# A hybrid attention and retention layer: one set of four transposes a group for dilation 1, and moved loads and splits at the stage borders

## The chip, the cores and the metric

The kernel runs on one core of a Trainium2 chip. The metric is the device time of one execution in microseconds (us). The core has five engines with an instruction queue each, which work in parallel and wait for one another by semaphores: TensorE (PE in the profile; its weight loads PEld), VectorE (DVE), ScalarE (ACT), GpSimd (POOL) and SyncE (SP), which only issues transfers. DVE, ACT and PE can reach PSUM, the memory that TensorE writes; in this kernel POOL works on SBUF alone.

## The reference

One layer for 4096 positions of width 1024, in float32. The input is normalised (RMS) and projected; of the result, eight heads of 64 go through dilated sliding-window attention, four heads through retention. Both are gated (SiLU), joined, projected and added to the input, and a last RMS norm follows. What the change touches is one branch of the attention, and how the branches are joined:

```python
DILATED_BRANCHES = ((128, 1), (512, 4), (2048, 16))      # (window, dilation)
...
    s = jnp.einsum('bhrnqd,bhrnkd->bhrnqk', qb, kb) * (Dh ** -0.5)
    dist = steps + qi - kj
    band = (dist >= 0) & (dist <= steps)
...
    p = jnp.exp(s - m)
    den = jnp.sum(p, axis=-1, keepdims=True)
    o = jnp.einsum('bhrnqk,bhrnkd->bhrnqd', p, vb) / den
    lse = (m + jnp.log(den))[..., 0]
...
    w = jax.nn.softmax(jnp.stack(lses, axis=0), axis=0)
    o = jnp.sum(w[..., None] * jnp.stack(outs, axis=0), axis=0)
```

Each block of 128 queries sees its own 128 keys (distance 0 and up) and the 128 before them (distance down to and including 128 steps). Since the branches are weighted by their denominators, the joined output is a sum over all three branches of unnormalised weights times v, divided by the sum of these weights. For a query and a key column of the same number, the key in the own block is at distance 0, that in the block before at distance 128; for every other column exactly one of the two is inside the window of dilation 1.

## The kernel before

The work has three stages, and each engine's instructions stand in the order in which the code issues them (`manual_schedule`).

**Projections** (`phase1`, line 115). Blocks of 512 positions are multiplied by the weights; each float32 operand is split into a high and a low part, so that `mm3` (lines 44 to 50) makes three matmuls of one product. Rotated q, k and v go to DRAM (`dr_q`, `dr_k`, `dr_r`, `dr_v`). For the last block the first loads of the next stage are issued in between: chunk 0 of the input (`load_x_chunk`, line 423), k of head 0 (`load_k`, lines 439 to 447), and chunk 1.

**Attention and retention** (`phase2`, line 544). Attention goes through 8 heads of 24 groups: 4 of dilation 1, 8 of dilation 4, 8 of dilation 16, 4 of dilation 1, so that eight groups of dilation 1 stand together at each change of head. A group is four blocks of 128 queries in two banks of two. `attention()` (line 818) issues one bank a slot: the scores S of a bank (`qk_bank`, 667); one slot later the exponentials on ACT (`exp_row`, 695) with the negated maxima that DVE found (`row_max`, 688, which also adds the mask); one more slot later four transposes of P on TensorE (`t_bank`, 704; three where there is no block before) and the copy of the transposed bank into the tile `pt`, bank 0 by DVE (716), bank 1 by ACT (714); at the fourth slot after the group's first the products with v (`pv_group`, 737), and then ACT's copy of the output. For dilated groups q is gathered four slots ahead, one half on POOL and one on DVE (643, 648). In each group the tile `pt` holds eight 128x128 blocks: for each block of queries the transposed weights of the block before and of the own block.

Between the slots `filler()` (1021) puts pieces of work by their TensorE cost: for each of 32 chunks of 128 positions the retention (scores 923, outputs, state, group norm 982 to 1002) and a part of the V products (L48 to L50 with tile V, whose epilogue `vch` is line 1037). It brings work to POOL (`hc`, the low part of the input chunk, 435; `rkl`, 908; `qbd`, 911; `qg`, 937; `rs`, 999) and to DVE and ACT. At the end gate weights are split (`split`, 76 to 88) and the first gates run.

**Output** (`phase3`, line 1134). For blocks of 256 positions: gates (`gate`, 1182, exponential in 1190), the joined and weighted attention (`mix`, 1193 to 1217), the split of the result (38 to 41), the output projection with `wo`, and the last norm. The weights of the branches (`branch_weights`, 498 to 528) come from the maxima and denominators of all heads, which `end_head` transposes into the tile `st`, `store_stats` (783) writes to DRAM (`dr_st`) and `load_stats` (786 to 796) reads back, three slots later, into `raw`. In its first steps `start()` (1255) also splits the eight parts of `wo`.

Two lines of the tables matter below: masks are tables with 0 inside and a large number outside the window; `row_max` takes the minimum of the negated scores plus mask, so that adding a negative number to a mask's entry makes the weight larger.

## Time and profile before

| | |
|---|---|
| time, median of 3 runs | 2415.1 us (2414.91 to 2417.89) |
| the profiled execution | 2416.7 us, its span 2414.9 us |
| granted TensorE clock, mean | 0.988 |
| transposes of P (line 704) | 1368 |
| exponentials (line 695) | 768 |
| DMA | 362.59 MB, mean 150 GB/s |

The profile is one execution seen by the hardware profiler. Busy times are sums of instructions' lengths on an engine; a busy TensorE is one that has matmuls in flight, and two matmuls that follow each other overlap, so a price per matmul is read from the distance between starts. In a timeline each row gives start, busy time, engine, line, operation, what is written from what, and the count; a bracket gives the idle time of that engine just before and who ended it. In a list of waits the columns are the total, the number and the longest. A row of a window gives its length and the busy time of each engine in it.

### The profile page before, as it was taken

The page shows a single profiled execution, that of the slowest core. Times are in us where ns is not written, and L with a number is a line of the kernel's source. Part 1 is how long each engine was busy: PE and PEld are TensorE (multiplying, and loading weights), DVE is VectorE, ACT ScalarE, POOL GpSimd, SP SyncE. Part 2 cuts the span into 40 slices and gives each one's busy share as a digit, 9 for nine tenths or more (in the row PEclk, how much of TensorE's full clock was granted, in tenths as well). Part 3 has the DMA queues.
Part 4 walks back from the last instruction along what each step waited for, and adds up shares of the span by engine and source line. Part 5 has one row for each costly group of instructions (what it writes and reads, how often), then busy time and mean ns, then how long its engine had stood idle before and what let it go on. Part 6 is the DMA issues. An engine that isn't in the chain of part 4 may idle for free. (4 is left out here: it accounts for less than half of the span.)

```text
span 2414.9 us, 41800 instructions
## 1 busy us (share of the span) xinstructions
PE 2342.5 (97%) x14568; PEld 1986.1 (82%) x14568; DVE 1485.8 (62%) x3923; ACT 990.0 (41%) x2865; POOL 725.0 (30%) x765
## 2 busy tenths in 40 slices
PE   7999999999997999999999999998899999999998
PEld 5778888888885888888888887877789899999997
DVE  5643543543534878787887879786665565665654
ACT  4322222222211666666666666667222222222221
POOL 5312112112112535353544535455221121121110
PEclk9999999999998999999999999999999999999999
DMA  6343343343356766758586765746575656656553
GB/s 192 130 145 107 133 144 107 133 144 111 129 147 202 165 163 139 181 131 189 131 180 148 169 156 131 176 125 196 143 182 154 145 171 152 145 168 154 142 153 92
DMA packets 404259, 362.59 MB, mean 150 GB/s; under 512 B 191848, under 2 KB 334824, under 8 KB 398928
## 3 DMA queue, kind: packets, MB, share of 16 engines
q1 hardware_dynamic: 389408, 332.91, 52.6%
q10 hardware_dynamic: 14112, 25.43, 3.4%
q8 instruction: 115, 1.88, 0.3%
q0 software_dynamic: 528, 1.58, 0.2%
q14 instruction: 96, 0.79, 0.1%
HBM read 241.18 MB, written 118.64 MB: 149 GB/s over the span
## 5 line engine op out<-in xcount | busy, mean ns | idle before, releaser
L688 DVE CUSTOM_DVE_ANT_0 S<-S,mask 128x256 f32<-128x256 f32 (+1 forms) x768 | 308.4, 402 | 156.7 <-PE S L667 123.5
L695 ACT ACTIVATE P<-S,nm 128x256 f32<-128x256 f32 (+1 forms) x768 | 337.2, 449 | 46.9 <-DVE nm L688 43.9
L50 PE MATMUL g<-h,wg 128*128 128x256 f32 x1024 | 290.6, 284 | 0.0
L704 PE MATMUL T<-ident,P 128*128 128x128 f32 x1368 | 213.3, 274 | 0.0
L49 PE MATMUL po<-wo,m 128*128 128x512 f32 x512 | 200.6, 392 | 0.0
L50 PEld LDWEIGHTS g<-h,wg 128*128 128x128 f32 x1024 | 197.1, 192 | 0.0
L737 PE MATMUL O<-pt,v 128*64 128x128 f32 (+1 forms) x1968 | 195.8, 325 | 0.0
L667 PE MATMUL S<-kk,qc 128*128 128x256 f32 x1024 | 186.9, 306 | 6.8 <-issue 2.8
L48 PE MATMUL po<-wohi,m 128*128 128x512 f32 x448 | 178.9, 399 | 6.9 <-ACT m L40 5.4
L1251 POOL TENSOR_TENSOR rs<-v,mhalf 128x1 f32<-128x1 f32 x32 | 17.5, 547 | 547.0 <-DVE v L1249 384.9
L667 PEld LDWEIGHTS S<-kk,qc 128*128 128x128 f32 x1024 | 150.0, 191 | 34.7 <-issue 17.5
L50 PE MATMUL po<-wohi,m 128*128 128x512 f32 x448 | 176.9, 396 | 0.2 <-DVE m L41 0.2
L172 POOL TENSOR_TENSOR sq<-sq,sq 128x512 f32<-128x512 f32 x56 | 76.3, 1362 | 331.4 <-ACT sq L168 331.4
L435 POOL TENSOR_TENSOR hc<-hr,hc 128x512 fp32r<-128x512 f32 x64 | 85.9, 1343 | 289.3 <-ACT hc L434 149.6
L737 PEld LDWEIGHTS O<-pt,v 128*64 128x64 f32 x1968 | 121.2, 137 | 60.3 <-issue 31.2
L704 PEld LDWEIGHTS T<-ident,P 128*128 128x128 f32 x1368 | 163.8, 141 | 0.2 <-ACT wg0hi L87 0.2
L695 ACT ACTIVATION_READ_ACCUMULATOR P<-S,nm 128x1 f32 x768 | 157.5, 205 | 0.0
L48 PE MATMUL g<-h,wg1hi 128*128 128x256 f32 x512 | 145.9, 286 | 4.6 <-ACT e L1190 4.5
L40 ACT ACTIVATE m<-e 128x256 fp32r<-128x256 f32 x128 | 53.1, 417 | 234.5 <-DVE e L1197 137.8
L49 PE MATMUL g<-h,wg1hi 128*128 128x256 f32 x512 | 146.9, 287 | 0.9 <-DVE h L483 0.7
L48 PE MATMUL g<-h,wg0hi 128*128 128x256 f32 x512 | 144.8, 283 | 1.8 <-ACT e L1190 1.8
L49 PE MATMUL g<-h,wg0hi 128*128 128x256 f32 x512 | 144.9, 283 | 0.0
(212 smaller groups left out, 6120.7 us busy)
## 6 DMA issues: line engine op xcount, KB each, us to landing
q<-dr_q SPq DMA_DIRECT2D x128, 256.0 KB
hr<-in_xT_dram SPq DMA_DIRECT2D x64, 512.0 KB
wb<-dr_w SPq DMA_DIRECT2D x128, 192.0 KB
o<-dr_o SPq DMA_DIRECT2D x192, 128.0 KB
v<-dr_v SPq DMA_DIRECT2D x94, 256.0 KB
xt<-in_xT_dram SPq DMA_DIRECT2D x64, 256.0 KB
dr_q<-hl SPq DMA_DIRECT2D x32, 512.0 KB
dr_k<-hl SPq DMA_DIRECT2D x32, 512.0 KB
```

The source lines that it names most:

```text
L40: nc.scalar.activation(dst[:, 0], src, AF.Copy)
L48: nc.tensor.matmul(out, wh, xh, start=first and i == 0, stop=False)
L49: nc.tensor.matmul(out, wh, xl, start=False, stop=False)
L50: nc.tensor.matmul(out, wl, xh, start=False, stop=last and i == n - 1)
L172: nc.gpsimd.tensor_tensor(sums[b], sums[b], sq, ALU.add)
L435: nc.gpsimd.tensor_tensor(hc[:, :, 1, :], src, hc[:, :, 0, :].bitcast(F32), ALU.subtract)
L667: nc.tensor.matmul(s[:, j * 256 : (j + 1) * 256], qq[h, t, half][:, off : off + 128] if br == 0 else it["q"][:, t, i, :], rhs, start=(j == ...
L688: nc.vector.tensor_tensor_reduce(sv, sv, mask[:, it["br"], c0:256], 1.0, BIG, ALU.add, ALU.min, accum_out=nm[:, col : col + 1])
L695: nc.scalar.activation(it["P", i // 2][:, i % 2, c0:256], sv, AF.Exp, bias=nm[:, col : col + 1], scale=-1.0, accum_out=den[:, col : col + 1])
L704: nc.tensor.transpose(t[:, j * 128 : (j + 1) * 128], it["P", bank][:, j // 2, j % 2 * 128 : j % 2 * 128 + 128], ident)
L737: nc.tensor.matmul(o[64 * bank : 64 * bank + 64, c0 : c0 + 128 * m], vt[h, br, idx // 8][:, idx % 8, :], it["pt"][:, a : a + m, :].rearran ...
L1251: nc.gpsimd.tensor_tensor(rs, v, mhalf, ALU.pow)
```

## The change

1. Groups of dilation 1, except the last two of the last head, are `one` (62 groups). Their two halves, the own block and the block before, get masks that exclude each other: the distance of 128 steps is taken out of dilation 1's mask and given to dilation 4 as a doubled weight (its mask entry becomes -ln 2: the key at distance 128 is in that branch's window too). `merge` then adds the two halves of P, bank 0 on DVE, bank 1 on POOL; `t_merged` transposes the four sums instead of eight (or seven) halves; `t_apart` takes them apart in the transposed tile: ACT copies the 128x512 block out of PSUM and POOL multiplies it by an upper triangle, DVE multiplies it from PSUM by a lower triangle. For these groups transposing comes one slot later for bank 1 and two for bank 0, and the products with v two slots later. P has five buffers instead of three. The triangles come from the mask, with one transpose on TensorE; the new mask of dilation 4 is made by two selections on POOL.
2. The first load of k goes by GpSimd's queue.
3. The tile `st` lives in a pool that outlasts the stage, and so does the tile `rb` of the scales; for the last head `load_stats` is issued by ACT's queue in the first steps of the output stage.
4. In the output stage POOL makes the low parts of all seven `wo` splits (DVE made every other one), and in the attention's end DVE makes the high parts of the last gate weights (ACT made them). Two loads of heads in the first output block go by GpSimd's queue.

The core of the diff (the masks and triangles, the new functions, and where they are issued):

```diff
@@ phase1 @@
-                kk = load_k(nc, kka, dr, 0, cols=slice(0, S - BLK))
+                kk = load_k(nc, kka, dr, 0, nc.gpsimd.dma_start, cols=slice(0, S - BLK))
@@ phase2 @@
-        pp = pool("p2p", 3)
+        pp = pool("p2p", 5)
...
+        nc.vector.tensor_scalar(mask[:, 0, :128], mask[:, 0, 128:], -1.0, BIG, ALU.mult, ALU.add)
+        for half, far in ((0, 128), (1, 0)):
+            mv = mask[:, 1, half * 128 : half * 128 + 128]
+            nc.gpsimd.affine_select(
+                out=mv,
+                in_=mv,
+                compare_op=ALU.not_equal,
+                fill=-float(np.log(2.0)),
+                base=32 - far,
+                pattern=[[32, 4], [1, 4], [4, 8]],
+                channel_multiplier=-1,
+            )
+
+        tri = cp.tile([128, 2, 128], F32, name="tri2")
+        nc.vector.tensor_scalar(tri[:, 1, :], mask[:, 0, 128:], 0.0, None, ALU.is_equal)
+        trit = psT.tile([128, 512], F32, tag="T", name="tri2")
+        nc.tensor.transpose(trit[:, :128], tri[:, 1, :], ident)
+        nc.vector.tensor_copy(tri[:, 0, :], trit[:, :128])
+        nc.vector.tensor_scalar(tri[:, 1, :], trit[:, :128], -1.0, 1.0, ALU.mult, ALU.add)
...
+        def merge(it, bank):
+            a = 1 if it["blocks"][2 * bank][1] == 0 else 0
+            P = it["P", bank]
+            (nc.gpsimd if bank else nc.vector).tensor_tensor(P[:, a:, 128:], P[:, a:, 128:], P[:, a:, :128], ALU.add)
+
+        def t_merged(it):
+            t = psT.tile([128, 512], F32, tag="T", name="T2")
+            for i in range(4):
+                nc.tensor.transpose(t[:, i * 128 : (i + 1) * 128], it["P", i // 2][:, i % 2, 128:], ident)
+            it["T"] = t
+
+        def t_apart(it, part):
+            t = it["T"].rearrange("p (b q) -> p b q", b=4)
+            same, prev = it["pt"][:, :4], it["pt"][:, 4:]
+            low, up = (tri[:, i].unsqueeze(1).broadcast_to([128, 4, 128]) for i in range(2))
+            if part:
+                nc.vector.tensor_tensor(same, t, low, ALU.mult)
+            else:
+                nc.scalar.activation(prev, t, AF.Copy)
+                nc.gpsimd.tensor_tensor(prev, prev, up, ALU.mult)
...
+                it["slot"] = 2 * len(items) + (6 if it["one"] else 5 if items and items[-1]["one"] else 4)
...
+                im, bm = half(t - 4)
...
+                im = im if im and im["one"] and not bm else None
+                ready, i2 = (i2, None) if i2 and i2["one"] else (None, i2)
+                if im:
+                    t_merged(im)
+                    cost += 4 * TRN
...
+                if im:
+                    t_apart(im, 0)
                 if i2 and b2:
                     t_copy(i2, b2)
...
+                if im:
+                    t_apart(im, 1)
+                if ready:
+                    merge(ready, b2)
...
-            st = r1.tile([96, 256], F32, tag="st", name="st2")
+            st = ahead["st"].tile([96, 256], F32, tag="st", name="st2")
...
-            later(3, load_stats, h)
+            if h < H - 1:
+                later(3, load_stats, h)
+            else:
+                ahead["stats"] = lambda: load_stats(h, nc.scalar.dma_start)
@@ phase3 @@
-            for _ in range(3):
+            for i in range(3):
+                if i == 2:
+                    ahead["stats"]()
                 yield
...
-                wo7.split(j, None if j % 2 else nc.gpsimd)
+                wo7.split(j, nc.gpsimd)
@@ early3 @@
-                wg[0].split(k, nc.gpsimd)
+                wg[0].split(k, nc.gpsimd, nc.vector)
```

Where this moves instructions is seen in the queues. Line numbers of the new code are some 3 higher up to line 557 and 23 to 80 higher behind it. SP at the passage from the projections to the attention, before (hr are chunks of the input, kk is the tile of k, hl are rotated k on their way to DRAM):

```order
L423 DMA hr_5113<-in_xT_dram 128x8x128
L445 DMA kk_5115<-dr_k 32x3584 x4
L259 DMA dr_k<-hl_5130 128x2x512
L259 DMA dr_k<-hl_5134 128x2x512
L423 DMA hr_5144<-in_xT_dram 128x8x128
L445 DMA kk_5115<-dr_k 32x512 x4
L1362 DMA rgain_5324<-in_ret_gain_dram 128x4
```

and now:

```order
L426 DMA hr_5113<-in_xT_dram 128x8x128
L262 DMA dr_k<-hl_5130 128x2x512
L262 DMA dr_k<-hl_5134 128x2x512
L1436 DMA rgain_5324<-in_ret_gain_dram 128x4
L426 DMA hr_5144<-in_xT_dram 128x8x128
L448 DMA kk_5115<-dr_k 32x512 x4
```

The large load of kk is gone from SP, and the load of rgain stands ahead of the second hr instead of behind the rest of kk. POOL at the same place, before (ident and mask are constants, rq and rk the first retention chunk):

```order
masks.py:197 MEMSET ident_5374 128x128
L572 DMA mask_5379<-in_masks_dram 128x768
masks.py:199 AFFINE_SELECT ident_5374<-ident_5374 128x128
L574 DMA decay_5381<-in_decayT_dram 128x512
L576 DMA qdec_5383<-in_qdec_dram 128x256
L578 DMA kdec_5385<-in_kdec_dram 128x4
L580 DMA cdec_5387<-in_cdec_dram 128x2
L897 DMA rq_5401<-dr_r 128x2x128
L897 DMA rk_5403<-dr_r 128x2x128
```

and now:

```order
L448 DMA kk_5115<-dr_k 32x3584 x4
L438 TENSOR_TENSOR hc_5138<-hr_5113,hc_5138 128x4x128
L438 TENSOR_TENSOR hc_5141<-hr_5113,hc_5141 128x4x128
masks.py:197 MEMSET ident_5374 128x128
L575 DMA mask_5379<-in_masks_dram 128x768
masks.py:199 AFFINE_SELECT ident_5374<-ident_5374 128x128
L577 DMA decay_5381<-in_decayT_dram 128x512
L579 DMA qdec_5383<-in_qdec_dram 128x256
L581 DMA kdec_5385<-in_kdec_dram 128x4
L583 DMA cdec_5387<-in_cdec_dram 128x2
L590 AFFINE_SELECT mask_5379<-mask_5379 128x128 x2
L968 DMA rq_5414<-dr_r 128x2x128
```

POOL issues the load of kk first, and the two selections on the mask stand between the loads of the constants and those of rq and rk. POOL at a change of head, in the attention, from the last groups of dilation 1 to the first gathers for dilation 4 (hc, rkl, qbd, qg and rs belong to the chunk work, qc are gathers), before:

```order
L435 TENSOR_TENSOR hc_8463<-hr_8349,hc_8463 128x4x128
L908 TENSOR_TENSOR rkl_8590<-rk_8413,rkh_8589 128x256
L911 TENSOR_TENSOR qbd_5395<-rq_8411,qbd_5394 64x2x128 x2
L643 COPY qc_8603<-q_00_8241 128x512
L435 TENSOR_TENSOR hc_8669<-hr_8349,hc_8669 128x4x128
L643 COPY qc_8685<-q_01_8476 128x512
L937 TENSOR_TENSOR qg_5397<-rq_8411,qdec_5383 64x2x128 x2
L999 TENSOR_TENSOR rs_8663<-rs_8663,mhalf_5389 128x4
L643 COPY qc_8746<-q_00_8241 128x512
```

and now:

```order
L763 TENSOR_TENSOR pt_5404<-pt_5404,tri_5398 128x512
L746 TENSOR_TENSOR P_8558<-P_8558 128x2x128
L1008 TENSOR_TENSOR qg_5410<-rq_8379,qdec_5383 64x2x128 x2
L1070 TENSOR_TENSOR rs_8577<-rs_8577,mhalf_5389 128x4
L666 COPY qc_8665<-q_01_8453 128x512
L763 TENSOR_TENSOR pt_5405<-pt_5405,tri_5398 128x512
L746 TENSOR_TENSOR P_8627<-P_8627 128x2x128
L666 COPY qc_8729<-q_00_8213 128x512
L763 TENSOR_TENSOR pt_5404<-pt_5404,tri_5398 128x512
L746 TENSOR_TENSOR P_8697<-P_8697 128x2x128
L438 TENSOR_TENSOR hc_8773<-hr_8655,hc_8773 128x4x128
L666 COPY qc_8784<-q_01_8453 128x512
```

Additions (L746) and multiplications by the triangle (L763) now stand among the chunk work and the first gathers, in the order of the slots. ACT at the passage from the attention to the output, before (st and raw hold the statistics, e are gates, m their product's high part):

```order
L779 ACTIVATE st_17656<-Ts_17653 96x256
L87 ACTIVATE wg0hi<-raw_17444 128x512
L752 ACTIVATE os_17683<-O_17658 128x256
L1163 DMA rt_17748<-dr_ret 128x256
L1163 DMA rt_17771<-dr_ret 128x256
L1190 ACTIVATE e_17773<-g_17512 128x256
L1190 ACTIVATE e_17777<-g_17551 128x256
L40 ACTIVATE m_17779<-e_17773 128x256
L40 ACTIVATE m_17787<-e_17777 128x256
L1190 ACTIVATE e_17785<-g_17587 128x256
L1190 ACTIVATE e_17823<-g_17798 128x256
```

and now:

```order
L831 ACTIVATE st_17549<-Ts_17546 96x256
L804 ACTIVATE os_17551<-O_17522 128x256
L1235 DMA rt_17640<-dr_ret 128x256
L1235 DMA rt_17663<-dr_ret 128x256
L1262 ACTIVATE e_17665<-g_17392 128x256
L804 ACTIVATE os_17578<-O_17553 128x256
L1262 ACTIVATE e_17669<-g_17439 128x256
L40 ACTIVATE m_17671<-e_17665 128x256
L845 DMA raw_5321<-dr_st 16x2x256
L40 ACTIVATE m_17679<-e_17669 128x256
L1262 ACTIVATE e_17677<-g_17473 128x256
L847 DMA raw_5321<-dr_st 16x4x64
```

The loads of raw from dr_st now stand in ACT's queue, after the first gates and among the multiplications, and the last high parts of the gate weights (wg0hi) have left ACT.

More of the change, by code (lines that the diff above doesn't have):

```diff
@@ L733, in pv_group @@
                         continue
[L734 removed]
+                    r, n, slots, c0 = ops[bank][x]
+                    m = len(range(8)[slots])
                     idx = r * NB_OF[br] + n
@@ L812, in phase2 @@
                 it["pt"] = PT[len(items) % 2]
+                it["one"] = br == 0 and not (h == H - 1 and gi >= len(groups) - 2)
+                it["slot"] = 2 * len(items) + (6 if it["one"] else 5 if items and items[-1]["one"] else 4)
                 items.append(it)
@@ L1075, in phase2 @@
         per_head = sum(
-            872 + TRN * (8 - sum(it["blocks"][2 * i][1] == 0 for i in range(2))) + pv_cost(it) for it in items[: len(groups)]
+            872 + TRN * (4 if it["one"] else 8 - sum(it["blocks"][2 * i][1] == 0 for i in range(2))) + pv_cost(it)
+            for it in items[: len(groups)]
         )
```

48 lines of the change are left out of this document (28 added, 20 removed).

## The prediction

> **What bounds the kernel now.** I read the page's busy times first, then the busy time by stage, then the waits of TensorE. The page's row of engines:
>
> ```profile
> PE 2342.5 (97%) x14568; PEld 1986.1 (82%) x14568; DVE 1485.8 (62%) x3923; ACT 990.0 (41%) x2865; POOL 725.0 (30%) x765
> ```
>
> TensorE is busy for all but 72 of the 2414.9 us. Whether that holds in the stage that the change touches is seen by stage; the columns are the length, then busy time of each engine, then the granted clock, the DMA share and the rate:
>
> ```profile
> core 0: us, PE busy (x) PEld busy (x) DVE busy (x) ACT busy (x) POOL busy (x), PEclk, DMA share, GB/s
> 750.00:850.00 100.00, 82.93 (x583) 69.61 (x582) 60.31 (x208) 44.40 (x150) 45.79 (x54) 0.91 0.69 176
> 850.00:1450.00 600.00, 598.16 (x4702) 502.89 (x4702) 474.59 (x1761) 412.07 (x1425) 265.10 (x304) 1.00 0.68 158
> ```
>
> From 850 to 1450, the attention stage, TensorE has 598 of 600 us at full clock: a TensorE instruction taken out there shortens the run, as long as nothing else takes its place. It has 83 of 100 us around the passage into this stage; its waits name that gap and those of the passage out of it (total, times, longest):
>
> ```profile
> PE V L48 <- DVE vch L1037: 16.5, 1, 16.5
> ...
> PE S L667 <- ACT P L695: 7.8, 10, 2.3
> PE g L48 <- ACT e L1190: 6.3, 2, 4.5
> PE po L48 <- ACT m L40: 5.4, 1, 5.4
> ```
>
> **The attention stage: what goes.** 62 groups give up half of their transposes, and the seven-transpose first group of each head gives up three: 62 x 4 - 8 = 240 of 1368. The group's row says 274 ns for one, but these matmuls overlap, so the price is the distance between starts, read from a stretch of TensorE's timeline (start, length, name, count):
>
> ```profile
> L704 PE MATMUL T<-ident,P 128*128 128x128 f32 x1368 | 213.3, 274 | 0.0
> ...
> 1002.02 0.60 PE L704 MATMUL T<-ident,P 128*128 128x128 f32 x4
> 1002.55 1.09 PE L737 MATMUL O<-pt,v 128*64 128x128 f32 x12
> ...
> 1004.15 0.60 PE L704 MATMUL T<-ident,P 128*128 128x128 f32 x4
> 1004.59 0.60 PE L1015 MATMUL Rt<-ident,on 128*128 128x128 f32 x4
> ```
>
> Four transposes take 0.53 us to the next product and 0.44 us to the next transposes, so 0.11 to 0.13 us each. 240 x 0.11 = 26.4 us; at 0.13 it is 31. I take **-27 us**. The products with v keep their number and width, only the tile's slots differ, so they cost what they did.
>
> **The attention stage: what comes.** Each of the 62 groups gets one addition of 128x256 on DVE, one on POOL, and a multiplication of 128x512 on POOL. DVE's multiplication out of PSUM stands where the copy of bank 0 stood, and ACT's copy where that of bank 1 stood, each of 128x512 as before: those I cost at nothing. The nearest rows for the three new ones, and for what DVE's addition may cost beside a busy POOL (line 170, two SBUF inputs; shortest, median, longest):
>
> ```profile
> L1208 DVE TENSOR_TENSOR a<-a,u 128x256 f32<-128x256 f32 x64 | 26.9, 420 | 0.6
> ...
> L908 POOL TENSOR_TENSOR rkl<-rk,rkh 128x256 fp32r<-128x256 f32 x32 | 26.4, 824 | 174.1 <-DVE rkh L907 120.3 <-PE Ro L958 28.0 <-PE S L667 14.7
> ...
> L435 POOL TENSOR_TENSOR hc<-hr,hc 128x512 fp32r<-128x512 f32 x64 | 85.9, 1343 | 289.3 <-ACT hc L434 149.6 <-DVE hc L432 54.6 <-DVE on L1002 20.5
> ```
>
> ```profile
> L170 DVE TENSOR_TENSOR h<-xt,h x64: 666/866/1778, 8.8 to 664.8; 128x512 fp32r<-128x512 f32 x64
> ```
>
> So DVE +0.42 us a group, and for the upper end double, 0.84 (line 170 goes from 666 ns to 1778, with a median of 866); POOL 0.82 + 1.34 = +2.16 us a group. Eight such groups stand together at each change of head. Busy times of seven of these stretches, one of them and the sum with its mean:
>
> ```profile
> 984.00:1020.00 36.00, 36.00 (x294) 30.69 (x293) 28.06 (x106) 25.72 (x88) 13.93 (x16) 1.00 0.86 193
> ...
> sum 256.00, PE 255.01 PEld 214.66 DVE 194.46 ACT 180.50 POOL 87.72; mean PE 36.43 PEld 30.67 DVE 27.78 ACT 25.79 POOL 12.53
> ```
>
> A stretch is 256 / 7 = 36.6 us. Without the transposes TensorE needs 36.6 - 31 x 0.11 = 33.2. DVE goes to 27.8 + 8 x 0.42 = 31.2, or at the doubled price 34.5; POOL to 12.5 + 8 x 2.16 = 29.8. So TensorE still has the most to do, but POOL is at 90% and DVE at 94% of its time, and each POOL addition stands between an exponential and the next slot's transposes: with the chunk work of POOL ahead of it in its queue it will sometimes be late. Bounds: nothing, if all fits; 62 / 8 x (34.5 - 33.2) = 10 us, if DVE sets the pace; 21 us, if in each of the eight stretches two low parts of hc (2 x 1.34) stand ahead of an addition and TensorE waits for all of it. I take **+9 us**, close to the middle one, since two engines so near to full do not interleave without loss.
>
> The GPSIMD Engine Reference of the Trainium skill (Specifications) says of GpSimd's SBUF interfaces that they are shared with VectorE, with contention where a DVE instruction has two SBUF inputs; the new DVE additions are such instructions. The trace agrees by line 170's spread. By that rule alone the stretch would be DVE's 34.5 us and this term +10; by the undisturbed row it would be nothing.
>
> The gate weights' high parts that DVE takes from ACT at the attention's end, and the loads of heads by GpSimd's queue, I cost at nothing: TensorE waits on ACT's exponentials for 7.8 us in ten places, so a lighter ACT can win up to 3 there, and DVE's eight casts fall where the chunk work has run out.
>
> **The passage from projections to attention.** The rows of SP, the loads' landing times, and DVE, POOL and TensorE there:
>
> ```profile
> 735.76 18.08 SPq L445 DMA_DIRECT2D kk<-dr_k  x4
> 761.79 2.72 SPq L259 DMA_DIRECT2D dr_k<-hl  x2
> 767.95 0.37 SPq L423 DMA_DIRECT2D hr<-in_xT_dram  x1
> ...
> 754.05 0.06 DVE L1365 MEMSET mhalf<- 128x1 f32 x1 [2.39 <-PE mm L50]
> ...
> 778.36 0.43 DVE L432 CAST hc<-hr 128x512 fp32r<-128x512 f32 x1 [10.47 <-DMA hr<-in_xT_dram]
> ...
> 742.95 3.06 POOL L435 TENSOR_TENSOR hc<-hr,hc 128x512 fp32r<-128x512 f32 x2 [45.88 <-DVE hc L432]
> ...
> 757.18 0.78 POOL L572 DMA_DIRECT2D mask<-in_masks_dram  x1
> ...
> 768.67 1.51 POOL L911 TENSOR_TENSOR qbd<-rq,qbd 64x256 fp32r<-64x256 f32 x2
> 778.92 1.27 POOL L435 TENSOR_TENSOR hc<-hr,hc 128x512 fp32r<-128x512 f32 x1 [8.75 <-DVE hc L432]
> ...
> mask<-in_masks_dram POOLq DMA_DIRECT2D x1, 384.0 KB, 5.7
> ...
> rq<-dr_r POOLq DMA_DIRECT2D x1, 128.0 KB, 6.1
> ```
>
> ```profile
> 757.30 0.50 PE L48 MATMUL V<-w2hi,hc 128*128 128x512 f32 x1 [0.60 <-ACT vo L273]
> ...
> 762.65 0.39 PE L50 MATMUL V<-w2hi,hc 128*128 128x512 f32 x1
> 779.50 0.79 PE L48 MATMUL V<-w2hi,hc 128*128 128x512 f32 x1 [16.47 <-DVE vch L1037]
> 780.10 0.63 PE L49 MATMUL V<-w,hc 128*128 128x512 f32 x1
> 780.52 0.63 PE L50 MATMUL V<-w2hi,hc 128*128 128x512 f32 x1
> ```
>
> The second chunk hr is issued at 767.95, behind the k loads and the k stores, lands at 778.36, and only then do DVE's cast and vch run, for which TensorE has waited. On POOL the k loads fall into 45.88 us of idleness (four issues of some 0.8 us, as the mask's), so they cost nothing. On SP the gain row now stands ahead of hr and waits for the memory that comes free when TensorE is done with the projections, 754.05; hr lands 10.4 us after that, 764.5 (its own transit before, 778.36 - 767.95). What is late next: the transpose that builds the masking tile. It waits for the mask, 757.18 + 5.7 = 762.9, and two small DVE steps, so 763.5, and on TensorE it stands ahead of the first chunk's V products, which until now ran from 757.30 to 762.65, 24 of them 0.23 us apart. After such a gap they are 0.42 apart (780.10 to 780.52; the granted clock of this stage was 0.91): at that price for the first dozen and 0.23 for the rest they end near 771.5. POOL's two selections wait for the same mask and push rq to 763.6, landing 6.1 later, 769.7; then POOL's work on rk and rq (0.82 and 1.51), with DVE's casts ahead of it, and the low part of hc (1.27) end at about 774.5, where they ended at 778.92 + 1.27 = 780.2. So TensorE's V products of chunk 1 run 5.7 us earlier: **-6 us**. Ends: 0, if the mask or POOL is later still; -13, if TensorE is held by neither.
>
> **The passage from attention to the output.** SP, ACT, DVE and POOL there:
>
> ```profile
> 1667.33 0.77 SPq L783 DMA_DIRECT2D dr_st<-st  x1
> ...
> 1674.47 0.66 ACT L1190 ACTIVATE e<-g 128x256 f32<-128x256 f32 x2 [6.37 <-DMA dr_st<-st]
> ...
> 1696.96 1.23 DVE L88 TENSOR_TENSOR wo<-wo,wohi 128x1024 fp32r<-128x1024 f32 x1 [2.50 <-POOL wo L88]
> 1698.10 3.02 DVE L1197 SCALAR_TENSOR_TENSOR e<-rt,rgain,e 128x256 f32<-128x256 f32 x2
> ...
> 1698.32 2.52 POOL L88 TENSOR_TENSOR wo<-raw,wohi 128x1024 fp32r<-128x1024 f32 x1 [1.39 <-DVE wo L88]
> ```
>
> With st in a pool that lives on, the first gates' exponential no longer waits for its store: the stall of 4.5 us goes. But the loads of the statistics now stand in ACT's queue and wait there for the same store (1674.5), with multiplications and exponentials of the next gates queued behind them; part of the wait comes back at the third or fourth gate. The second stall (5.4 us, line 40 behind DVE at 1698.10) ends earlier by DVE's freed splits (three of 1.23), while POOL gets three more of 2.5. I take half of the two stalls: **-5 us**. Ends: -12, both gone (9.9) with 2 of slow clock; +3, if POOL's 3 x 2.5 come in the place of the 4.5 that goes.
>
> **The sum.** The profiled execution took 2416.7 us, 1.8 of it outside its span, and 1.6 above the median of 2415.1. -27 + 9 - 6 - 5 = -29, so 2387.7 for that execution and **2386 us** for the median.
>
> **Rivals.**
> 1. *POOL sets the pace (slower).* In POOL's queue the pair of qg, rs, a gather and a multiplication by the triangle stand between two additions of a stretch, as its rows at a change of head show. If every addition of bank 1 comes 0.9 us after TensorE wants it (two thirds of a step of 1.34 that began just before it), that is 62 x 0.9 = 56 us against the 38 of gains: 2415 - 38 + 56 = 2433. It decides from 38 / 62 = 0.61 us a group. For it: 90% on POOL. Against: the sum of POOL's work fits in the 33.2 us, and half of the groups have no chunk work ahead. Chance 0.11.
> 2. *The passages bring nothing.* The masking tile's wait and the cold clock take up the earlier hr, and ACT's loads the earlier e: -27 + 9 = -18, 2397. For it: each passage has a new wait of about the old length. Chance 0.21.
> 3. *The attention stage keeps nothing.* DVE at the doubled price (10) and late additions on POOL (21) come together and use up the 27: only the passages' 11 are left, 2404; chance 0.13. For it: the two engines' 94% and 90%. Against: from 850 to 1450 as a whole DVE has 79% and POOL 44%, so late chunk work can be made up in the rest of a head. With passages that bring nothing as well, 2415, no difference to be measured: 0.07.
>
> The page DMA: Bandwidth & Descriptors of the Trainium skill (Issuing engines are not separate DMA queues) says that a DMA issued from another engine runs on the same 16 DMA engines and saves only the issuing time. It speaks for rival 2. SP's row of 18.08 us at 735.76, with hr behind it, is far more issuing time than such a saving is taken to be.
>
> **How the numbers follow.** The forecast has 0.48. Its own range, with half of each term's bounds, is 2376 to 2396. Down to -27 - 13 - 12 + 4 = -48 (2367) the bounds of both passages reach with half of the stage's price; upward I take in rivals 2 and 3, to 2408. Left out are rival 1 and the case of no difference, 0.18. A measurement of this kernel tells about 0.2%, 4.8 us, from no change. Faster: 0.48 + 0.21 + 0.13 = 0.82; within: 0.07; slower: 0.11.
>
> **What would show it.** Right: 1128 transposes in the L704 and merged groups together; TensorE still 98% or more in the dil-1 stretches, each near 34.4 us; hr landed by 766 and the V products of chunk 1 before 776; the first e some 4 us earlier against its gate, with no wait on the store. Wrong: waits of TensorE's merged transposes on POOL's additions of over 20 us in total; DVE or POOL over 97% in those stretches; a gap ahead of the first chunk's V products longer than the 16.5 us that it replaces.

## The result and the profile after

The changed kernel takes 2458.0 us (median of 4 runs) beside 2415.0 for the kernel before on the same chip: a ratio of 1.0178, 95% interval 1.0157 to 1.0198. It is 43 us slower, where 29 us faster was forecast and the range ended at 2408. The profiled execution took 2454.0 us, 4 below that median, with a span of 2452.2 and a mean granted clock of 0.980 (before 2414.9 and 0.988). The page's engines:

```profile
PE 2344.7 (96%) x14329; PEld 1974.0 (80%) x14329; DVE 1545.7 (63%) x3994; ACT 990.6 (40%) x2857; POOL 872.9 (36%) x900
```

There are 239 TensorE instructions fewer and just as much TensorE time: 2344.7 us against 2342.5, and 107.5 us idle in the span against 72.4. The groups of transposes have shrunk as counted, 880 + 248 = 1128, and from 213.3 to 139.9 + 44.7 = 184.6 us:

```profile
L727 PE MATMUL T<-ident,P 128*128 128x128 f32 x880 | 139.9, 274 | 1.9 <-DVE pt L739 1.9
L752 PE MATMUL T<-ident,P 128*128 128x128 f32 x248 | 44.7, 285 | 34.8 <-POOL P L746 29.3 <-DMA raw<-dr_st 3.4 <-DVE rs L1068 1.2
```

The other matmuls take some 31 us more. A clock lower by 0.8% would make about 19 of that (estimate: 0.008 x 2342). To see where the 37.3 us of the span come from, take the first and the last row maximum of the attention in VectorE's timeline (start, length, name), of before and of after:

```profile
786.08 0.30 DVE L688 CUSTOM_DVE_ANT_0 S<-S,mask 128x128 f32<-128x128 f32 x1 [1.63 <-PE S L667]
...
1660.31 0.43 DVE L688 CUSTOM_DVE_ANT_0 S<-S,mask 128x256 f32<-128x256 f32 x1
```

```profile
782.41 0.30 DVE L711 CUSTOM_DVE_ANT_0 S<-S,mask 128x128 f32<-128x128 f32 x1 [2.50 <-PE S L690]
...
1691.23 0.43 DVE L711 CUSTOM_DVE_ANT_0 S<-S,mask 128x256 f32<-128x256 f32 x1
```

| us of the profiled execution | before | after | difference | forecast |
|---|---|---|---|---|
| to the first maximum | 786.1 | 782.4 | -3.7 | -6 |
| first to last maximum | 874.2 | 908.8 | +34.6 | -18 |
| last maximum to the end | 754.6 | 761.0 | +6.4 | -5 |
| span | 2414.9 | 2452.2 | +37.3 | -29 |

Cut at the first maximum of each dilation's groups (768 rows like these, four to a group), the 34.6 us lie in the groups of dilation 1 for the most part: the first four of the eight heads take 168.6 us together instead of 147.7, the last four of seven heads 133.0 instead of 124.9, and those of the last head 27.5 instead of 20.6. The groups of dilation 4 take 6.9 us more in all, those of dilation 16 take 8.3 less.

From the first to the last maximum, before and after, and in the last head's final four groups, after (length, busy time of PE, PEld, DVE, ACT and POOL, clock, DMA share, rate):

```profile
786.08:1660.31 874.23, 861.35 (x6756) 723.50 (x6755) 701.04 (x2571) 598.51 (x2059) 408.04 (x459) 1.00 0.66 156
...
782.41:1691.23 908.82, 856.19 (x6503) 703.98 (x6502) 753.69 (x2636) 600.13 (x2054) 540.39 (x583) 0.98 0.63 150
...
1664.00:1692.00 28.00, 18.06 (x101) 14.88 (x100) 16.37 (x51) 13.65 (x43) 20.26 (x20) 0.70 0.21 62
```

TensorE has only 5.2 us less work there, at a somewhat lower clock, and is idle for 52.6 us, where it was for 12.9. The 28 us of the last head's final groups are the worst place: 18.06 busy, at a granted clock of 0.70. The waits of TensorE (total, times, longest) name the releaser:

```profile
PE T L752 <- POOL P L746: 29.3, 21, 3.5
PE g L49 <- DVE h L486: 9.4, 5, 4.3
...
PE g L48 <- ACT e L1262: 5.1, 2, 4.0
```

The 29.3 us of merged transposes that wait for GpSimd's additions are the mark that the prediction set for being wrong (over 20). Another of its marks did not show: neither DVE nor POOL comes near 97% in the stretches (88% and 72%, from the sums further down). And the steps themselves have about the lengths that it used; the rows of the three new ones (shortest, median, longest, in ns):

```profile
L746 DVE TENSOR_TENSOR P<-P x62: 281/878/1418, 788.3 to 1678.8; 128x256 f32<-128x256 f32 x54, 128x128 f32<-128x128 f32 x8
L746 POOL TENSOR_TENSOR P<-P x62: 711/770/1145, 791.9 to 1684.4; 128x256 f32<-128x256 f32 x62
L763 POOL TENSOR_TENSOR pt<-pt,tri x62: 1261/1291/1707, 795.3 to 1686.4; 128x512 f32<-128x512 f32 x62
```

GpSimd's addition was taken at 0.82 and its multiplication at 1.34; VectorE's addition, taken at 0.42 with 0.84 as the upper end, has a median of 0.88. So the lengths are not what the forecast had wrong. What an addition waits for is seen in GpSimd's timeline at a change of head:

```profile
1353.37 0.72 POOL L746 TENSOR_TENSOR P<-P 128x256 f32<-128x256 f32 x1
1354.06 1.93 POOL L1008 TENSOR_TENSOR qg<-rq,qdec 64x256 f32<-64x256 f32 x2
1356.07 1.15 POOL L1070 TENSOR_TENSOR rs<-rs,mhalf 128x4 f32<-128x4 f32 x1
1357.16 1.13 POOL L666 CAST qc<-q 128x512 fp32r<-128x512 f32 x1
1358.23 1.71 POOL L763 TENSOR_TENSOR pt<-pt,tri 128x512 f32<-128x512 f32 x1
1359.90 0.72 POOL L746 TENSOR_TENSOR P<-P 128x256 f32<-128x256 f32 x1
```

and beside it in ACT's and TensorE's:

```profile
1353.74 0.46 ACT L718 ACTIVATE P<-S,nm 128x256 f32<-128x256 f32 x1
...
1354.68 0.60 ACT L762 ACTIVATE pt<-T 128x512 f32<-128x512 f32 x1 [0.38 <-PE T L752]
```

```profile
1358.20 0.38 PE L752 MATMUL T<-ident,P 128*128 128x128 f32 x2
1360.67 0.44 PE L752 MATMUL T<-ident,P 128*128 128x128 f32 x2 [2.09 <-POOL P L746]
```

The group's last exponential (the row at 1353.74) ended at 1354.20, and the addition of bank 1 could have run from then on. But ahead of it in the queue stood the previous group's multiplication, whose input ACT had copied by 1355.28, itself behind three rows of chunk work and gathers (qg, rs, qc). So the addition began only at 1359.90, and TensorE stood still for 2.09 us. This is no exception: chunk steps ran on GpSimd between the group's last exponential and its addition of bank 1 in 43 of the 62 groups, a multiplication in 53, and the addition began 3.4 us after that exponential in the median (counted in ACT's and GpSimd's timelines). Here it was the chunk steps that held the multiplication. There is a second dependence: the multiplication needs ACT's copy, which needs the previous group's transposes, which need the previous addition: a round through one queue, once a group. Lateness in GpSimd's queue, by chunk steps or by the round, is the first theory for the runs. Its rivals: the additions and the multiplication cost by their sheer time, on GpSimd or on VectorE; the planner (`filler()`) fills the time freed on TensorE with chunk work, which then lengthens every engine's stretch; and the passages, not the stage, lose the time.

### The profile page after: what moved, and what is told of

The parts are those of the page before. It is cut to its first block, busy times and chain, and to the rows that moved or that the text cites. A ratio compares the mean times of both kernels' runs of the same rounds, so it can differ in the third digit from the quotient of the medians.

```text
span 2452.2 us, 41502 instructions
## 1 busy us (share of the span) xinstructions
PE 2344.7 (96%) x14329; PEld 1974.0 (80%) x14329; DVE 1545.7 (63%) x3994; ACT 990.6 (40%) x2857; POOL 872.9 (36%) x900
## 5 line engine op out<-in xcount | busy, mean ns | idle before, releaser
L1323 POOL TENSOR_TENSOR rs<-v,mhalf 128x1 f32<-128x1 f32 x32 | 17.7, 554 | 545.6 <-DVE v L1321 510.5
L1262 ACT ACTIVATE e<-g 128x256 f32<-128x256 f32 x128 | 48.4, 378 | 233.4 <-PE g L50 216.1
L727 PE MATMUL T<-ident,P 128*128 128x128 f32 x880 | 139.9, 274 | 1.9 <-DVE pt L739 1.9
```

The costliest lines, as they stand in the source:

```text
L727: nc.tensor.transpose(t[:, j * 128 : (j + 1) * 128], it["P", bank][:, j // 2, j % 2 * 128 : j % 2 * 128 + 128], ident)
L1262: nc.scalar.activation(e, g[:, :TB], AF.Silu)
```

## The experiments

Ratios are to the kernel before, with 95% intervals. "Length" is the time from first to last maximum in the profiled execution, 874.2 before and 908.8 after.

### Which half of the change loses the time

Both additions on VectorE (1); the upper triangle by VectorE straight from PSUM, without ACT's copy and GpSimd's multiplication (2); no merged groups, all else as changed (3); merged groups alone, all passages as before (4):

```diff
1 -(nc.gpsimd if bank else nc.vector).tensor_tensor(P[:, a:, 128:], ...
1 +nc.vector.tensor_tensor(P[:, a:, 128:], ...
2 -nc.scalar.activation(prev, t, AF.Copy)
2 -nc.gpsimd.tensor_tensor(prev, prev, up, ALU.mult)
2 +nc.vector.tensor_tensor(prev, t, up, ALU.mult)
3 -it["one"] = br == 0 and not (h == H - 1 and gi >= len(groups) - 2)
3 +it["one"] = False
4 -kk = load_k(nc, kka, dr, 0, nc.gpsimd.dma_start, cols=slice(0, S - BLK))
4 +kk = load_k(nc, kka, dr, 0, cols=slice(0, S - BLK))
4  (and st, rb, load_stats, wo7.split, wg[0].split, the heads' loads as before)
```

> The changed kernel with both additions of the halves on VectorE; GpSimd keeps only the multiplication by the triangle. Theory Q (GpSimd's queue): in the dil-1 stretches and just behind them GpSimd has more than its time (additions, multiplications, chunk work, first gathers), the addition of bank 1 comes late, TensorE waits for it (29.3 us in 21 places) and then runs on a slower clock. With 0.82 us a group less on GpSimd and no transposes waiting for it, the time falls to about 2420 to 2435. Theory V (VectorE is as full): the 62 additions of 0.82 us only move to an engine at 94%, TensorE waits for VectorE instead, and the time stays at 2450 or above. Theory P (the passages are to blame): stays at about 2455.

> The changed kernel with the upper triangle multiplied by VectorE straight out of PSUM (0.69 us) in place of ScalarE's copy and GpSimd's multiplication (1.34 us); the addition of bank 1 stays on GpSimd. Theory Q: GpSimd loses 1.34 of its 2.16 us a group, its additions come in time, the waits of the merged transposes on GpSimd go from 29 us to below 8, and the time falls to about 2400 to 2425, also because an addition on VectorE beside a less busy GpSimd is shorter (0.42 rather than 0.82). Theory V: VectorE gets 0.69 us a group more and sets the pace, 2445 or above. Theory P: about 2455.

> The changed kernel with no merged groups: eight transposes a group as before (the masks stay disjoint), but with all the changes of the two passages. Theories Q and V: the loss is in the attention stage, so this run lies near the kernel before: -4 us from the first passage, and the second at -5 to +6, in all 2405 to 2420. Theory P: the second passage with its 7 us of loss and the last head with its 7 are due to the moved loads and splits, 2420 to 2430.

> The changed kernel with merged groups, but with the passages as before: k of the first head on SyncE's queue, the statistics' tile and loads, the splits of the gate and output weights as they were. Theories Q and V: 2450 to 2462, the passages add little. Theory P: 2435 to 2445.

| run | median us | ratio | length |
|---|---|---|---|
| 1 | 2451.9 | 1.0139 (1.0124 to 1.0155) | 904.5 |
| 2 | 2449.1 | 1.0124 (1.0107 to 1.0141) | 908.0 |
| 3 | 2422.0 | 1.0026 (1.0014 to 1.0038) | 875.0 |
| 4 | 2448.6 | 1.0131 (1.0110 to 1.0152) | 907.4 |

The merged groups are the loss: alone +33 us, without them +6. (Runs 1 and 2 come out as theory V said; run 3 lies 2 us above the range of Q and V and in that of P, run 4 between the two ranges.) In run 4 the wait has hardly moved, so the passages don't make it:

```profile
PE T L752 <- POOL P L746: 31.6, 22, 3.2
```

Giving VectorE either of GpSimd's steps gains 6 to 9 us and no more; the wait takes another name. Run 1, then run 2:

```profile
PE T L752 <- DVE P L746: 15.9, 23, 2.2
```

```profile
PE S L690 <- ACT P L718: 28.8, 33, 3.7
```

### Is it the planner's chunk work?

In the seven stretches of eight merged groups at a change of head (first maximum of the last four groups to that of dilation 4), before and after:

```profile
sum 254.39, PE 253.40 PEld 212.99 DVE 194.81 ACT 178.84 POOL 87.08; mean PE 36.20 PEld 30.43 DVE 27.83 ACT 25.55 POOL 12.44
```

```profile
sum 277.96, PE 255.25 PEld 207.09 DVE 243.92 ACT 183.20 POOL 199.58; mean PE 36.47 PEld 29.58 DVE 34.85 ACT 26.17 POOL 28.51
```

A stretch grew from 36.3 to 39.7 us, where 34.4 was forecast. TensorE's work in it has not shrunk at all, although the 31 transposes are gone: its timeline shows 692 chunk matmuls in the seven stretches, and 534 before. The planner fills what is freed. So runs 5 and 6 (on run 4) charge a merged group 8 and 14 transposes instead of 4, which sends chunk work elsewhere:

```diff
5, 6 -cost += 4 * TRN
5    +cost += 8 * TRN
6    +cost += 14 * TRN
     (and the same number where a head's cost is summed)
```

> Merged groups with the passages as before (2448.6), but the planner charges a merged group eight transposes (as it did before) though it makes four, so that the chunk work is spread over the slots as it was before. Theory F (the planner fills the freed TensorE time of the merged slots with chunk work, which brings VectorE's and GpSimd's steps along): the chunk matmuls of the seven stretches at the changes of head go back from some 690 to some 530, the stretches from 39.7 to about 35 us, the waits of the merged transposes on GpSimd from 32 us to below 12, and the time to 2410 to 2425. Theory V (VectorE and GpSimd are too slow for the added steps wherever the chunk work lies; an addition costs VectorE 0.8 us beside GpSimd): 2440 or above.

> As the last, but a merged group is charged fourteen transposes, so that some 5 us of TensorE's chunk work leave each stretch of eight merged groups and go to the dilated groups. Theory F: stretches of about 30 us, no waits on GpSimd's additions to speak of, dilated groups longer than before by what went there; the saving of the transposes is kept, 2388 to 2405. Theory V: little better than with eight, 2435 or above. If the dilated stretches become full instead (they hold the gathers), 2405 to 2425.

Run 5: 2448.2 us, ratio 1.0142 (1.0123 to 1.0160), length 905.4. Run 6: 2461.1 us, 1.0196 (1.0177 to 1.0214), length 916.7. The stretches of run 5, then of run 6:

```profile
sum 265.12, PE 242.63 PEld 193.82 DVE 238.91 ACT 178.66 POOL 193.54; mean PE 34.66 PEld 27.69 DVE 34.13 ACT 25.52 POOL 27.65
```

```profile
sum 267.44, PE 237.09 PEld 185.57 DVE 228.23 ACT 173.52 POOL 182.27; mean PE 33.87 PEld 26.51 DVE 32.60 ACT 24.79 POOL 26.04
```

The chunk matmuls there go down to 608 and 486, and a stretch to 37.9 and 38.2 us, but the rest of the head gets the work back: no gain at 8, a loss at 14. The observation stands, the theory built on it falls.

### Which of the passages' edits costs 6 us?

On run 3: the `wo` splits in turn as before (7), and the statistics' tile, store and loads as before (8):

```diff
7 -wo7.split(j, nc.gpsimd)
7 +wo7.split(j, None if j % 2 else nc.gpsimd)
8 -st = ahead["st"].tile([96, 256], F32, tag="st", name="st2")
8 +st = r1.tile([96, 256], F32, tag="st", name="st2")
8 -ahead["stats"] = lambda: load_stats(h, nc.scalar.dma_start)   (and its call)
8 +later(3, load_stats, h)
```

> No merged groups, all changes of the passages (2422.0), except that the low parts of the output weights are split by VectorE and GpSimd in turn as before. If GpSimd's queue of wo splits makes the second passage 8 us longer (VectorE's low parts of h took 1.4 us each beside them, with TensorE waiting 7 us for the last), the time falls to 2412 to 2416; if the loads of the statistics in ScalarE's queue do it, it stays at 2419 to 2424.

> No merged groups, all changes of the passages (2422.0), except that the statistics' tile and its last load are as before (SyncE, three slots later). If the loads in ScalarE's queue make the second passage longer, 2411 to 2416; if the wo splits do it, no better than 2420, and perhaps 2 us worse, since the first exponential waits for the tile's store again.

Run 7: 2419.3 us, 1.0017 (1.0002 to 1.0031), 761.5 us after the last maximum; run 8: 2420.8 us, 1.0029 (1.0013 to 1.0045), 763.2; run 3 has 763.4 there and the kernel before 754.6. Neither gives the 9 us back, and the intervals of 3, 7 and 8 overlap: inconclusive as to which edit it is (more on this passage below). The casts of the gate weights on VectorE and the heads' loads by GpSimd's queue were not tried alone.

### The order of the steps

On run 4: GpSimd's addition one slot earlier, ahead of the previous group's multiplication (9); VectorE's read of the merged tile ahead of ACT's copy (10); both (11); both with 8 transposes charged (12); run 9 with 8 charged (13):

```diff
9, 11  +if i1 and i1["one"] and b1:
9, 11  +    merge(i1, 1)
9       if im:
9           t_apart(im, 0)
...
9, 11  -if ready:
9, 11  +if ready and not b2:
            merge(ready, b2)
...
10, 11  if im:
10, 11      t_apart(im, 1)
10, 11 +    t_apart(im, 0)      (and gone from above)
```

> Merged groups with the passages as before (2448.6), and on GpSimd the addition of bank 1 one slot earlier, ahead of the last group's multiplication by the triangle instead of behind it; nothing is left out. Theory F has fallen, so the new ones: Theory R (a round from group to group in GpSimd's queue): the addition's inputs are ready, but it stands behind a multiplication that waits for ScalarE's copy, which waits for the last group's transposes; these, the copy behind ScalarE's exponentials, the multiplication and the addition make one round of over 4.5 us a group, however little chunk work there is. With the addition ahead, the transposes wait for GpSimd below 8 us (32 now), time 2415 to 2432. Theory M (a round through PSUM: VectorE's multiplication waits for ScalarE's copy of the same tile, and the next maxima stand behind it): waits move to ScalarE's exponentials, time 2440 or above. Theory V (VectorE's and GpSimd's work as such): 2445 or above.

> Merged groups with the passages as before (2448.6), and VectorE reads the transposed tile first, ScalarE's copy after it, where it was the other way round. Theory M: VectorE's maxima no longer stand behind ScalarE's exponentials and copy, 2415 to 2435. Theory R: the copy and so GpSimd's multiplication and its addition come later still, 2448 to 2470. Theory V: about 2445.

> Both of the last two edits. Theories R and M together: 2395 to 2415, since both rounds are open. R alone: as with the addition first alone, 2415 to 2432. M alone: as with VectorE first alone, or better. V: 2440 or above.

> Both of these edits, and a merged group charged eight transposes, so that the chunk work stays spread as before. If the rounds were what bound the merged groups, the freed TensorE time now shows in their stretches: some 5 us better than with both edits alone, 2390 to 2410. Theory V: 2435 or above.

> The addition of bank 1 first (2433.2) and a merged group charged eight transposes. Theory F (chunk work in the merged slots), which could not show while the round through GpSimd's queue set the pace: 2415 to 2425. Theory V (VectorE and GpSimd with the added steps, wherever the chunk work lies): 2429 to 2437.

| run | median us | ratio | length |
|---|---|---|---|
| 9 | 2433.2 | 1.0066 (1.0044 to 1.0089) | 891.1 |
| 10 | 2474.7 | 1.0244 (1.0218 to 1.0270) | 931.8 |
| 11 | 2457.1 | 1.0170 (1.0148 to 1.0192) | 912.2 |
| 12 | 2458.6 | 1.0180 (1.0151 to 1.0209) | 915.1 |
| 13 | 2438.2 | 1.0096 (1.0081 to 1.0111) | 894.4 |

Run 9 moves one instruction within one queue and gains 15.5 us, 1 us above theory R's range; the wait is below 8, as R asked. The new place is ahead of the multiplication and of that slot's chunk steps, so the run shows that lateness in the queue costs time, and not which of the two held the addition. Its waits of TensorE:

```profile
PE S L690 <- ACT P L718: 15.5, 20, 2.9
...
PE O L789 <- POOL pt L763: 10.9, 16, 1.2
...
PE T L752 <- POOL P L746: 7.2, 9, 1.2
```

The wait for additions falls from 31.6 to 7.2; part of it comes back as products that wait for the multiplication (10.9) and scores that wait for exponentials. The groups of dilation 4 (287.7 us, 293.7 in run 4, 287.1 before) and the last head's final four (21.4, 27.6, 20.6) are nearly back where they were; the first four of the heads are not (166.6, 168.1, 147.7). Run 10 was meant to free VectorE, whose multiplication waits in the changed kernel for ACT's copy out of the same PSUM tile:

```profile
DVE pt L760 <- ACT pt L762: 10.2, 17, 1.3
```

Turned round, the wait is ACT's, and more than ten times as long:

```profile
ACT pt L762 <- DVE pt L760: 119.7, 54, 7.2
```

Runs 12 and 13 show again that the charge is not it.

### What is left: the steps themselves

On run 9: without GpSimd's multiplication (14), without VectorE's addition of bank 0 (15), products one slot later with a third `pt` (16), and a GpSimd copy in place of the multiplication (18). Run 17 does without the multiplication by other arithmetic: the tile's sum of halves times v, plus VectorE's half times the difference of v and its neighbour block, which GpSimd forms once per 8 blocks; it also loads k by GpSimd's queue, as the change does.

```diff
14 -nc.gpsimd.tensor_tensor(prev, prev, up, ALU.mult)
15 -merge(ready, b2)            (bank 0; bank 1 stays)
16 -it["slot"] = 2 * len(items) + (6 if it["one"] else ...)
16 +it["slot"] = 2 * len(items) + (7 if it["one"] else ...)
16 -it["pt"] = PT[len(items) % 2]
16 +it["pt"] = PT[len(items) % 3]
17 -ops = [(r, n, slice(i, i + 6, 5), 0), (r, n + 1, slice(i + 1, i + 2), 128)]
17 +ops = [(-1, n, slice(i, i + 1), 0), (r, n, slice(i + 5, i + 6), 128), (-1, n + 1, slice(i + 1, i + 2), 128)]
17 +nc.gpsimd.tensor_tensor(d[:, 1:, :], v[:, 1:, :], v[:, :7, :], ALU.subtract)   (d is what slot -1 reads)
18 -nc.gpsimd.tensor_tensor(prev, prev, up, ALU.mult)
18 +nc.gpsimd.tensor_copy(prev, prev)
```

> The addition of bank 1 first (2433.2), without GpSimd's multiplication by the upper triangle (left out: the weights of the block before keep the own block's). It frees 83 us of GpSimd and takes away the products' wait for it (10.9 us). Theory G (GpSimd's multiplication is what is left): 2405 to 2415, and VectorE's additions take 0.45 to 0.6 us rather than 0.82. Theory V with VectorE alone: 2424 to 2432.

> The addition of bank 1 first (2433.2), without VectorE's addition of bank 0 (left out: two of four blocks lose the weights of the block before). It frees some 50 us of VectorE. Theory V: the maxima come earlier, ScalarE's exponentials and so the scores no longer wait (15.5 us), 2412 to 2420. Theory G: 2425 to 2433.

> The addition of bank 1 first (2433.2), and the products with v of a merged group one slot later, with a third tile for the transposed weights; nothing is left out. Theory G in its mild form (GpSimd's multiplication comes in time if it is given 2 us more): the products' waits of 10.9 us go, 2420 to 2426. Theory V: no better than 2430, since the lateness only moves on.

> A whole version without the multiplication by the upper triangle: the block before gets the unmasked sum of both halves times v of that block, and the own block gets its masked half times the difference of the two blocks' v, which GpSimd makes once for eight blocks (32 times about 1.6 us in place of 62 times 1.35); one more matmul a bank. The addition of bank 1 first, the passages as before but for k of the first head on GpSimd's queue. If GpSimd's multiplication is what holds the merged groups (2412.8 without it), 2405 to 2418; if two-input steps on GpSimd cost whatever their number, 2420 to 2430.

> The addition of bank 1 first (2433.2), and GpSimd copies the block onto itself in place of multiplying it by the triangle (left out: the mask; one SBUF input in place of two, about 1.2 us in place of 1.35). If it is GpSimd's time in the queue (additions and products waiting for it): 2426 to 2432, with VectorE's additions at 0.7 to 0.8 us. If it is the hold of a two-input step on VectorE's SBUF reads: 2413 to 2422, and VectorE's additions at 0.42 to 0.5 us.

| run | median us | ratio | length |
|---|---|---|---|
| 14 | 2412.8 | 0.9992 (0.9983 to 1.0001) | 874.1 |
| 15 | 2424.3 | 1.0040 (1.0025 to 1.0055) | 877.9 |
| 16 | 2446.9 | 1.0130 (1.0113 to 1.0147) | 906.5 |
| 17 | 2420.1 | 1.0021 (1.0012 to 1.0030) | 887.6 |
| 18 | 2416.9 | 1.0002 (0.9993 to 1.0012) | 874.5 |

Without the multiplication 20.4 us go, in theory G's range; without VectorE's addition 8.9, between the ranges of V and G. The multiplication slows VectorE too. Its addition in run 9 and in run 14 (shortest, median, longest):

```profile
L746 DVE TENSOR_TENSOR P<-P x62: 281/721/1311, 789.9 to 1668.9; 128x256 f32<-128x256 f32 x54, 128x128 f32<-128x128 f32 x8
```

```profile
L746 DVE TENSOR_TENSOR P<-P x62: 281/417/1310, 789.3 to 1651.2; 128x256 f32<-128x256 f32 x54, 128x128 f32<-128x128 f32 x8
```

Run 18 was to tell GpSimd's time from this hold on VectorE, by a step of the same time with one input. It doesn't, because the copy takes half the time:

```profile
L763 POOL COPY pt<-pt x62: 600/612/1050, 799.7 to 1659.5; 128x512 f32<-128x512 f32 x62
L746 DVE TENSOR_TENSOR P<-P x62: 282/428/1299, 792.6 to 1655.0; 128x256 f32<-128x256 f32 x54, 128x128 f32<-128x128 f32 x8
```

VectorE's addition is hardly disturbed (0.43 in the median) and 16.3 us are gained, but the queue is 0.7 us a group shorter as well. Run 16 was to take the products' wait away and made the scores wait longer instead:

```profile
PE S L690 <- ACT P L718: 30.6, 42, 3.3
```

Even run 14, without the multiplication, keeps none of the saved transposes: its stage is as long as before (874.1). TensorE's work in it falls by 17.7 us (843.7 against 861.35, at a clock of 0.99), but its idle time rises by as much. The scores wait longer for exponentials, 18.1 us where it was 7.8:

```profile
PE S L690 <- ACT P L718: 18.1, 24, 3.3
```

Run 17 needs care: its stage is 13.4 us longer than before, and its first maximum comes at 776.1, 9.9 us earlier, with the load of k moved; so its median alone does not say what its merged groups cost. No version that computes everything beats the kernel before; run 17, the best with merged groups, is 0.21% slower, and run 7, without them, 0.17%.

## Why the prediction was wrong, step by step

**"I take -27"** held in its count, 240 transposes fewer, and is not shown as time: TensorE's work from first to last maximum fell by 5.2 us, and by 17.7 in run 14, at a clock of 0.98 and 0.99 where it was 1.00. **The lengths of GpSimd's two steps** held; VectorE's addition is at the doubled price, which the prediction had as its upper end.

**"I take +9"** failed, and with it the forecast. The stage lost 34.6 where -27 + 9 was forecast, so what came cost 61.6 us, 0.99 a group, if the 27 were saved in full. TensorE's idle time there rose by 39.7 us, and 29.3 of it are waits for GpSimd's additions. The step that failed is the reason for a small price: "half of the groups have no chunk work ahead" and "the sum of POOL's work fits in the 33.2 us". The chunk steps ran ahead of the addition in 43 of 62 groups, and the sum (28.5 us a stretch, 29.8 forecast) did not tell how late it came. A sum of busy time says whether an engine can keep up, not whether an in-order queue delivers each result in time.

This is the mechanism of rival 1 (chance 0.11) in part. That its price, 0.9 a group, lies near the measured 0.99 is partly luck: TensorE waited for additions in 21 places and not in 62, and other costs make up the rest. The runs split the cost of the merged groups: run 4 is 33 us over before, and with the 27 saved that is 60; the order in the queue 15.5 (run 9), the multiplication 20.4 (run 14), VectorE's addition 8.9 (run 15). Some 15 remain, not separated, if the three add up, and some 6 if only run 14's 17.7 were saved. Whether the 20.4 are the multiplication's place in the queue or its hold on VectorE stays open. The forecast's upper bound for this term, 21 us, assumed two late steps of 1.34 in each stretch of eight groups; on average each group lost about a microsecond.

**"-6" for the first passage** was right in its mechanism, -3.7 in size in this pair of profiles. Over the runs, the six profiles with the whole new passage have the first maximum at 777.2 to 783.2, the thirteen with the old one at 781.5 to 786.8. SP, GpSimd and TensorE there, after:

```profile
754.99 0.39 SPq L426 DMA_DIRECT2D hr<-in_xT_dram  x1
```

```profile
774.51 1.26 POOL L438 TENSOR_TENSOR hc<-hr,hc 128x512 fp32r<-128x512 f32 x1
```

```profile
765.31 0.45 PE L603 MATMUL tri<-ident,tri 128*128 128x128 f32 x1 [8.07 <-DVE tri L601]
...
775.83 0.79 PE L50 MATMUL V<-w2hi,hc 128*128 128x512 f32 x1 [1.69 <-POOL hc L438]
```

The second chunk is issued at 754.99 (forecast 754.1), the masking tile's transpose follows at 765.31 (763.5), and GpSimd's low part ends at 775.8 (774.5): the products of the second chunk that need it start 4.7 us earlier than before. The links are 0.9, 1.8 and 1.3 us later than forecast.

**"-5" for the second passage** failed: +6.4 there, and +8.8 in run 3. It is no chance of one profile: the six profiles with the new passage have 761.0 to 765.3 us behind the last maximum, the fourteen with the old one 752.0 to 757.4, but for run 11 with 762.5. The prediction added up waits. The gate's exponential is still waited for (5.1 us in all, 6.3 before), the 5.4 us of line 40 are gone, and a wait of 9.4 us for h stands in their place. But the sum of the waits does not explain the loss. In the 100 us behind the last maximum TensorE is idle for 13.6 us before, 14.1 after and 12.8 in run 7; what differs is the granted clock:

```profile
1660.31:1760.31 100.00, 86.40 (x560) 76.06 (x560) 67.23 (x120) 41.75 (x88) 29.90 (x27) 0.95 0.64 172
...
1691.23:1791.23 100.00, 85.87 (x547) 76.99 (x547) 70.64 (x110) 39.18 (x82) 38.11 (x30) 0.90 0.64 163
...
1654.58:1754.58 100.00, 87.19 (x554) 76.72 (x553) 71.46 (x119) 38.66 (x82) 31.92 (x28) 0.91 0.67 170
```

That makes some 5 of the 6.4 us (estimate: 100 x (0.95 - 0.90)). What in the new order of the waits lowers the clock is not shown. What h waits for is seen in VectorE's timeline, before and then after, and in GpSimd's and TensorE's, after:

```profile
1689.60 3.60 DVE L528 TENSOR_TENSOR raw<-raw,M 32x256 f32<-32x256 f32 x3
```

```profile
1721.96 5.86 DVE L531 TENSOR_TENSOR raw<-raw,M 32x256 f32<-32x256 f32 x3
1727.85 11.39 DVE L486 SCALAR_TENSOR_TENSOR h<-hr,gain_all,h 128x256 fp32r<-128x256 f32 x8
```

```profile
1720.00 7.45 POOL L91 TENSOR_TENSOR wo<-wo,wohi 128x1024 fp32r<-128x1024 f32 x3 [2.43 <-ACT wohi L88]
...
1730.94 5.08 POOL L91 TENSOR_TENSOR wo<-wo,wohi 128x1024 fp32r<-128x1024 f32 x2
1736.10 2.46 POOL L91 TENSOR_TENSOR wo<-raw,wohi 128x1024 fp32r<-128x1024 f32 x1
```

```profile
1728.70 0.58 PE L49 MATMUL g<-h,wg1hi 128*128 128x256 f32 x1 [4.32 <-DVE h L486]
```

The longest wait, 4.32 us, ends as soon as VectorE comes to h: ahead of it stand the last steps of the branch weights, 5.86 us beside three `wo` subtractions in a row, 3.60 before. Then eight low parts of h take 11.39 / 8 = 1.42 us each beside GpSimd's work, three more of the seven subtractions among it; the median of all 128 is 0.48:

```profile
L486 DVE SCALAR_TENSOR_TENSOR h<-hr,gain_all,h x128: 471/479/2617, 1673.9 to 2375.6; 128x256 fp32r<-128x256 f32 x128
```

The prediction counted the 3 x 2.5 us that GpSimd gets and not what they do to VectorE. With the splits in turn (run 7) these eight take less than half,

```profile
1692.69 5.34 DVE L486 SCALAR_TENSOR_TENSOR h<-hr,gain_all,h 128x256 fp32r<-128x256 f32 x8
```

yet the clock stays at 0.91 and the time behind the last maximum at 761.5, so that edit alone is not shown to be the cause.

## What to carry to other kernels

When a step of a group moves to another engine, follow one group round: if its result stands in that engine's queue behind a step that needs the previous group's result, and that one behind chunk work, the wait can come back in group after group, however low the engine's busy share. Put what the bounding engine waits for ahead of what can wait: here one instruction moved by one slot was worth 15.5 us. A saving on the full engine (27 us by forecast) buys nothing if each of 62 groups gets three steps on a chain that was short before; charging the groups more, so that the background work goes elsewhere, did not bring it back here. When waits move and their sum stays, look at the granted clock before calling it even.

## What the runs showed of the hardware

- VectorE's steps with two SBUF inputs lengthen beside GpSimd's: the 128x256 addition has a median of 0.72 us in run 9 and 0.42 in run 14, the same kernel without GpSimd's multiplication (0.88 in the changed kernel). Where no step of GpSimd's ran at the same time, this addition took 0.41 to 0.42 in every run; in the changed kernel that was so for 1 of 54, in run 10, with the same multiplications issued later, for 27. The low part of h goes from 0.48 to 1.42. GpSimd's own 128x512 multiplication stays near 1.29 and reached 1.71 at most.
- GpSimd's copy of 128x512 in place takes 0.61 us, its multiplication of the same size 1.29, its cast of qc, of that size too, 1.13 in the row shown.
- Waits can cost twice: in the 28 us where TensorE was idle for 9.9, the longest of its waits for additions (3.5) among them, its granted clock was 0.70. The sum of idle time alone does not set the clock: behind the last maximum 13.6 us of idle time went with 0.95, and 14.1 with 0.90.
- Two engines that read one PSUM tile went one after the other in the order of issue: 10.2 us of waiting that way round, 119.7 the other. No run excludes that the program's semaphores for the tile, and not the chip, set this order.
